# Operands of a Winograd-style product: one by one for all tokens, on VectorE, with four units started ahead

## The chip, the cores and the metric

The kernel runs on one core of a Trainium2 chip. The metric is the device time of one execution in microseconds (us). The time before is 3162.38 us, the median of three runs.

The core's engines each work an instruction queue of their own in order: TensorE (PE in the rows; its weight loads are PEld), VectorE (DVE), ScalarE (ACT), GpSimd (POOL) and SyncE (SP), which here only issues DMAs. They wait for one another by semaphores.

## The reference

One transformer-like block of two different attentions, then a second block of two layers, over 1024 tokens of 1024 features, all in fp32. The change concerns the second block only, at the place where the mixer of a layer ends and its MLP begins:

```python
def sq_relu_mlp(h, w1, w2):
    return jnp.square(jax.nn.relu(h @ w1)) @ w2

for layer in range(DEPTH_2):                     # 2 layers
    if layer < N_A_LAYERS:
        mix = s5_mixer(h, ...)                   # ends in (val * sigmoid(gate)) @ w_out
    else:
        mix = mla_mixer(h, ...)                  # ends in o @ w_o
    h = layer_norm(DN_ALPHA * h + mix, ln_mix_g[layer], ln_mix_b[layer])
    h = layer_norm(DN_ALPHA * h + sq_relu_mlp(h, w_ff1[layer], w_ff2[layer]), ln_ffn_g[layer], ln_ffn_b[layer])
```

`w1` is 1024 x 4096 and `w2` is 4096 x 1024.

## The kernel before

**Precision.** Every fp32 matrix is used as two parts: a high part, rounded to the format that PE multiplies (fp32r), and the rest. `split` (L155 to L159) makes them: L157 copies the high part on ACT, L159 subtracts it from the source on an engine that the caller chooses (GpSimd if it names none). A product then takes three matmuls: high by high, high by low, low by high.

**`lin_ln`** (L1186) is the last projection of a layer's mixer. It goes over eight token tiles of 128 tokens, in two column halves `ch`. With the second half a tile's row is complete: it is added to the residual (L1215), normalized (`ln`, L1143 to L1154, the last step on DVE is L1154), written to memory (L1221) and transposed (`to_T4`: L1176 on PE, L1177 on ACT) into the pages `B[K, hf, pr]`: `K` is the feature half, `hf` the token half (tiles 0 to 3 or 4 to 7), `pr` one of two pairs of tiles in it. So for each `pr` there are four pages of 128 x 1024, called b11, b12 (K 0, the two token halves), b21, b22 (K 1).

**Seven products in place of eight.** The first MLP matmul is a 2 x 2 block product done with seven block products (Winograd's form of Strassen's method). The moving operands are sums of the blocks: X1 = b11, X2 = b21, X3 = b22, X5 = t1 = b12 - b11, X6 = t2 = b22 - t1, X7 = b22 - b12, X4 = b21 - t2. Each X[p] is kept for 512 tokens as a high and a low part in two pages of 256 features each (`split_T`), so each X takes, for each `pr`, two splits of 128 x 512 elements. X1 and X2 are split as soon as a pair of tiles of the first token half is done. The others are made after the last tile, in a loop over `pr` (L1236 to L1251): differences L1239, L1240 and L1244 on DVE and L1242 on GpSimd; the splits of X6, X5 and X4 on DVE, those of X1, X2, X7 and X3 on GpSimd.

**`ff1_unit`** (L1260) is a generator for one pair of feature tiles, 16 of which (*units*) make the first MLP matmul of a layer. A unit loads two weight pages of 512 KB: `r0` (L1293), whose split gives the weights of products 1 and 2, and `r1` (L1272), from which with `r0` the sums of `sums()` are made (L1273 to L1276 on DVE, their splits on ACT and GpSimd) for the other five. A product is 12 matmuls of 512 columns (`product`, L1257). Products 1 and 2 need X1 and X2 alone. The order of a unit's products is 1, 2, 6, 7, 5, 4, 3; L1304, L1308, L1317, L1323, L1327, L1332 and L1340 read their results from PSUM.

**Order.** Units 0 and 1 are started early inside `lin_ln`, at tiles 4 and 6, and do products 1 and 2 before the last operands are there (`early`); they use PSUM banks 4 and 5 for them. From unit 2 on, `ff1` (L1346) always starts the next unit's loads and sums while a unit is worked on. The code gives the engines' order only in part: Tile's scheduler may put an instruction ahead of others whose data come later. Pages come from a common list of free ones; a page that is given back is taken again by whoever asks next, who then waits for its last reader.

## Time and profile before

| | us |
|---|---|
| median of three runs | 3162.38 (3157.11 to 3164.09) |
| the profiled execution's own time | 3152.57 |
| its span | 3150.8 |
| PE busy | 3002.2 (95%) |
| DVE busy | 1705.4 (54%) |
| ACT busy | 1106.6 (35%) |
| POOL busy | 1464.0 (46%) |

The mean granted TensorE clock of the profiled execution is 0.98 of full speed. The change's two places in time are the transitions from `lin_ln` to `ff1`, at 1304 to 1350 us in layer 0 and at 2452 to 2498 us in layer 1. In the rows, a releaser behind `<-` names the instruction whose end let the waiting one start, and a group x24 counts 24 instructions that follow each other without another between them.

### The profile page before, as it was taken

To read this page: it belongs to the slowest core of one execution; us is meant where nothing else is said; L and a number is where in the kernel's file an instruction comes from. 1 tells how busy PE (TensorE), PEld (TensorE's weight loads), DVE (VectorE), ACT (ScalarE), POOL (GpSimd) and SP (SyncE) were. 2 spreads that over 40 slices of the span, in tenths; PEclk is the share of its full clock that TensorE was granted. 3 is DMA by queue.
4 is the path that set the end of the run, shared out by engine and by line. 5 is a ranking of instruction groups with operands and counts; after the bars stand their busy time and mean duration, and the time that the engine had idled before them with its cause. 6 is when DMAs were issued, how large, how long until landed. Compare 5 with 4: busy or idle time off the path is not lost.

```text
span 3150.8 us, 38281 instructions
## 1 busy us (share of the span) xinstructions
PE 3002.2 (95%) x14764; PEld 2473.2 (78%) x14764; DVE 1705.4 (54%) x2466; ACT 1106.6 (35%) x1723; POOL 1464.0 (46%) x871
## 2 busy tenths in 40 slices
PE   8999889999998899799999999999999799999998
PEld 6777667777777788678888888879998588888887
DVE  7555547755289301854444464765554854444446
ACT  4332247765223211332232221346562332232110
POOL 5455537644523232654455443513354654464442
PEclk9999999999999999899999999999999899999999
DMA  4353462476544122223363231111132133362211
GB/s 169 134 173 110 131 202 81 131 211 215 192 143 133 41 67 94 79 95 111 114 227 120 98 107 61 69 45 45 44 114 96 68 113 107 110 243 102 104 71 74
DMA packets 165014, 365.75 MB, mean 116 GB/s; under 512 B 21568, under 2 KB 70976, under 8 KB 164832
## 3 DMA queue, kind: packets, MB, share of 16 engines
q1 hardware_dynamic: 164688, 363.18, 34.0%
q8 instruction: 116, 1.90, 0.2%
q14 instruction: 66, 0.54, 0.1%
q10 hardware_dynamic: 144, 0.13, 0.0%
HBM read 248.70 MB, written 106.17 MB: 113 GB/s over the span
## 4 chain that ended last, share of the span: by engine, by line
PE 77%; DVE 12%; DMA 4%; POOL 2%; issue 2%; ACT 2%; SPq 1%; DVEq 0%; POOLq 0%; ACTq 0%
PE ps L172 56%; PE ps L1257 17%; DMA dr<-p 2%; POOL p L159 1%; DVE p L159 1%; DVE p L1032 1%; PE ps L1625 1%; DVE p L1045 1%; DMA p<-in_w_ff 1%; PE ps L668 1%; DVE p L498 1%; DVE p L1154 1%; PE ps L521 1%; POOL rsd L180 1%; ACT p L500 1%
## 5 line engine op out<-in xcount | busy, mean ns | idle before, releaser
L172 PE MATMUL ps<-p,p 128*128 128x512 f32 (+6 forms) x10520 | 2237.3, 373 | 63.1 <-POOL p L159 11.7
L172 PEld LDWEIGHTS ps<-p,p 128*128 128x128 f32 (+2 forms) x10520 | 1790.1, 185 | 438.4 <-issue 50.7
L159 POOL TENSOR_TENSOR p<-p,p 128x1024 fp32r<-128x1024 f32 (+2 forms) x436 | 982.3, 2274 | 955.3 <-ACT p L157 673.9
L157 ACT ACTIVATE p<-p 128x1024 fp32r<-128x1024 f32 (+2 forms) x462 | 423.9, 939 | 957.6 <-DMA p<-in_w_ff 452.9
L1257 PE MATMUL ps<-p,p 128*128 128x512 f32 x2688 | 622.1, 393 | 32.5 <-ACT p L157 31.6
L1257 PEld LDWEIGHTS ps<-p,p 128*128 128x128 f32 x2688 | 506.5, 189 | 146.6 <-ACT p L157 36.3
L1402 DVE SCALAR_TENSOR_TENSOR p<-ps,p 128x1024 f32<-128x1024 f32 x247 | 301.3, 1223 | 335.4 <-PE ps L172 335.4
L180 POOL TENSOR_TENSOR rsd<-rst,nhalf 128x1 f32<-128x1 f32 (+1 forms) x64 | 103.3, 1615 | 200.3 <-DVE rst L178 200.2
L1290 DVE SCALAR_TENSOR_TENSOR p<-p 128x512 f32<-128x512 f32 x96 | 96.9, 1010 | 2.5
L498 DVE CUSTOM_DVE_ANT_0 p<-ps,bw 128x1024 f32<-128x1024 f32 x64 | 77.3, 1220 | 30.6 <-PE ps L172 21.6
L1124 DVE SCALAR_TENSOR_TENSOR p<-p,ps 128x1024 f32<-128x1024 f32 x8 | 9.8, 1221 | 142.1 <-ACT p L1123 142.1
L500 ACT ACTIVATE p<-p,m 128x1024 f32<-128x1024 f32 x64 | 73.4, 1148 | 31.1 <-DVE m L498 19.5
L1619 POOL TENSOR_SCALAR p<-p,rz 128x256 f32<-128x256 f32 (+6 forms) x64 | 49.0, 766 | 65.3 <-DVE rz L1618 63.8
L1340 DVE TENSOR_TENSOR p<-p,ps 128x512 f32<-128x512 f32 x32 | 22.0, 688 | 104.5 <-PE ps L1257 104.4
L513 POOL TENSOR_TENSOR p<-p,p 128x1024 f32<-128x1024 f32 x32 | 76.9, 2407 | 2.0
L512 POOL TENSOR_SCALAR p<-p,c 128x1024 f32<-128x1024 f32 x32 | 37.2, 1163 | 84.8 <-DMA dr<-p 43.5
L1308 DVE TENSOR_TENSOR p<-p,ps 128x512 f32<-128x512 f32 x32 | 22.0, 686 | 97.2 <-PE ps L1257 97.0
L665 POOL TENSOR_SCALAR p<-p,rz 128x384 f32<-128x384 f32 x64 | 38.4, 604 | 68.8 <-DVE rz L664 54.2
L1629 DVE TENSOR_TENSOR p<-ps,p 128x512 fp32r<-128x512 f32 (+3 forms) x96 | 50.8, 553 | 32.5 <-ACT p L1628 31.8
L1614 POOL CAST p<-zeros 128x128 fp32r<-128x128 f32 x64 | 18.4, 298 | 105.4 <-PE ps L172 71.1
L159 DVE TENSOR_TENSOR p<-ps,p 128x1024 fp32r<-128x1024 f32 (+1 forms) x42 | 42.1, 1020 | 36.8 <-ACT p L157 34.0
L1177 ACT ACTIVATE p<-ps 128x512 f32<-128x512 f32 x32 | 17.8, 595 | 123.6 <-PE ps L1176 123.5
(255 smaller groups left out, 2420.2 us busy)
## 6 DMA issues: line engine op xcount, KB each, us to landing
p<-dr SPq DMA_DIRECT2D x174, 512.0 KB
dr<-p SPq DMA_DIRECT2D x158, 512.0 KB
p<-in_w_ff SPq DMA_DIRECT2D x128, 512.0 KB
bw<-in_rpbw SPq DMA_DIRECT2D x16, 768.0 KB
dr<-p SPq DMA_DIRECT2D x80, 128.0 KB
p<-p SPq DMA_DIRECT2D x64, 128.0 KB
p<-dr SPq DMA_DIRECT2D x32, 256.0 KB
p<-in_w_glu SPq DMA_DIRECT2D x16, 512.0 KB
```

The lines of the kernel that those rows point to most:

```text
L157: nc.scalar.activation(hi, src, AF.Copy, scale=scale)
L159: (eng or nc.gpsimd).tensor_tensor(lo, src, hi.bitcast(F32), SUB)
L172: self.nc.tensor.matmul(out, l, r, start=start, stop=stop)
L180: nc.gpsimd.tensor_tensor(dst, t, self.nhalf[:, :n], ALU.pow)
L498: V.tensor_tensor_reduce(out=s.t, in0=ps, in1=bw[:, 896 - 128 * t:1920 - 128 * t], scale=-1.0, scalar=3e38, op0=ADD, op1=ALU.min, accum_ou ...
L500: A.activation(s.t, s.t, AF.Exp, bias=m[:, c:c + 1], scale=-1.0, accum_out=z[:, c:c + 1])
L513: G.tensor_tensor(p[0].t, p[0].t, p[1].t, ADD)
L1257: self.nc.tensor.matmul(ps, w[a][:, kt, :], x[b][kt // 2].t[:, kt % 2, :], start=start and kt == 0 and (a, b) == (0, 0), stop=kt == 3 and ...
L1290: V.scalar_tensor_tensor(h, h, 0.0, h, ALU.max, MUL)
L1402: V.scalar_tensor_tensor(z[t].t, ps, IALPHA, z[t].t, MUL, ADD)
L1619: G.tensor_scalar(s.t[:, :n], s.t[:, :n], rz, 1.0, MUL, MUL)
L1629: V.tensor_tensor(atl[kq][:, :nb, qi * 128:(qi + 1) * 128], tv, oh.bitcast(F32), SUB)
```

## The change

The blocks b11 to b22 become lists over `pr`. A helper `op` makes one operand for both `pr` at once, first the two differences, then the four splits, in the order X6, X7, X5, X4, X3; t1 is made in place in b11. Everything that GpSimd did for the operands (X1, X2, X7 and X3's splits and the difference of X7) is done on DVE. Units 2 and 3 become early too: with units 0 and 1 they do products 1 and 2 inside `lin_ln`, in PSUM banks 4, 5, 0 and 1. The low part of units 2 and 3's first weights is made on DVE; an early unit gives `r0` back after its split and loads it a second time before `sums()`. In `ff1` units 1 to 3 make their sums when their turn comes, and the next unit's loads are started ahead from unit 4 on.

```diff
--- before.py
+++ after.py
@@ -1201,7 +1201,7 @@
         units = deque()
         for ch in range(2):
             ws = ws if ch == 0 else nat(1)
-            self.psum(**(dict(g1=[0, 1], tr=[2, 3], P=[4, 5], Q=[6, 7]) if ch else dict(g1=range(8))))
+            self.psum(**(dict(g1=[0, 1], tr=[2, 3], P=[4, 5, 0, 1], Q=[6, 7]) if ch else dict(g1=range(8))))
             for t in range(8):
                 ps = self.bank("g1")
                 hf, sl = t // 4, slice(t % 4 * 128, (t % 4 + 1) * 128)
@@ -1227,27 +1227,46 @@
                     self.fr(z[t])
                     if hf == 0 and t % 2:
                         for K in range(2):
-                            self.split_T(B[K, 0, pr].t, X, 1 + K, pr, G)
+                            self.split_T(B[K, 0, pr].t, X, 1 + K, pr, V)
                     if t in (4, 6):
                         units.append(self.ff1_unit(j, t // 2 - 2, X, True))
                         next(units[-1])
             self.fr(*(p for w in ws for p in w.pg))
         self.fr(*gb)
-        for pr in range(2):
-            b11, b12, b21, b22 = (B[K, hf, pr] for K in range(2) for hf in range(2))
-            t1, t2 = self.pg((128, 4, 256)), self.pg((128, 4, 256))
-            V.tensor_tensor(t1.t, b12.t, b11.t, SUB)
-            V.tensor_tensor(t2.t, b22.t, t1.t, SUB)
-            self.split_T(t2.t, X, 6, pr, V)
-            G.tensor_tensor(b12.t, b22.t, b12.t, SUB)
-            self.split_T(b12.t, X, 7, pr, G)
-            V.tensor_tensor(b21.t, b21.t, t2.t, SUB)
-            self.split_T(t1.t, X, 5, pr, V)
-            self.split_T(b21.t, X, 4, pr, V)
-            self.split_T(b22.t, X, 3, pr, G)
-            self.fr(b11, b12, b21, b22, t1, t2)
-            next(units[pr])
-            next(units[pr])
+        b11, b12, b21, b22 = ([B[K, hf, pr] for pr in range(2)] for K in range(2) for hf in range(2))
+        t2 = [self.pg((128, 4, 256)) for _ in range(2)]
+
+        def op(p, o, x, y):
+
+            for pr in range(2):
+                if y is not None:
+                    V.tensor_tensor(o[pr].t, x[pr].t, y[pr].t, SUB)
+            for pr in range(2):
+                if p:
+                    self.split_T(o[pr].t, X, p, pr, V)
+
+        def first(k):
+
+            for _ in range(2):
+                next(units[k])
+
+        op(0, b11, b12, b11)
+        op(6, t2, b22, b11)
+        first(0)
+        first(1)
+        op(7, b12, b22, b12)
+        self.fr(*b12)
+        for k in (2, 3):
+            units.append(self.ff1_unit(j, k, X, True))
+            next(units[k])
+            first(k)
+        next(units[0])
+        op(5, b11, None, None)
+        self.fr(*b11)
+        op(4, b21, b21, t2)
+        self.fr(*b21, *t2)
+        op(3, b22, None, None)
+        self.fr(*b22)
         return X, units
 
     def product(self, ps, w, x, start):
@@ -1292,7 +1311,9 @@
         r0 = self.pg()
         nc.sync.dma_start(r0.t, self.i["w_ff1"][layer, 2 * i])
         w0 = [self.pg(dt=F32R) for _ in range(2)]
-        self.split(r0.t, w0[0].t, w0[1].t)
+        self.split(r0.t, w0[0].t, w0[1].t, eng=V if early and i > 1 else None)
+        if early:
+            self.fr(r0)
         yield
         if not early:
             w23, w14, w4 = sums()
@@ -1310,6 +1331,8 @@
         self.fr(*w0)
         yield
         if early:
+            r0 = self.pg()
+            nc.sync.dma_start(r0.t, self.i["w_ff1"][layer, 2 * i])
             w23, w14, w4 = sums()
             yield
         self.product(P, [kv(w.t[:, lo]) for w in w23], X[6], False)
@@ -1345,13 +1368,13 @@
 
     def ff1(self, X, units, layer):
 
-        self.psb.update({"P": cycle([0, 1, 4, 5]), "R": cycle([2, 3])})
+        self.psb["R"] = cycle([2, 3])
         prev = None
         for i in range(16):
             u = units.popleft()
-            for _ in range(1 if i < 2 else 2):
+            for _ in range((0, 1, 1, 1)[i] if i < 4 else 2):
                 next(u)
-            nxt = self.ff1_unit(layer, i + 1, X, False, i == 14) if 0 < i < 15 else None
+            nxt = self.ff1_unit(layer, i + 1, X, False, i == 14) if 2 < i < 15 else None
             if nxt:
                 units.append(nxt)
                 next(nxt)
```

The new code has the operands' differences in line 1243, the product's matmuls in 1276, the first load of `r0` in 1312 and the second in 1335, `r1` in 1291, the weight sums in 1292 to 1295.

PE, layer 0, around the transposes (L1176) of the last token tile, whose normalized row is `p_888`. Before, unit 1's products (weights `p_925`, `p_926`) end there and unit 0's product 6 (operand `p_929`, `p_931`, weights `p_958`) comes next:

```order
L1257 MATMUL ps<-p_912_8999,p_926_9244 128x512
L1257 MATMUL ps<-p_912_8999,p_925_9243 128x512
L1257 MATMUL ps<-p_914_9001,p_925_9243 128x512
L1257 MATMUL ps<-p_912_8999,p_926_9244 128x512
L1176 MATMUL ps<-ident,p_888_8660 128x128 x8
L1257 MATMUL ps<-p_929_9294,p_958_9427 128x512
L1257 MATMUL ps<-p_931_9296,p_958_9427 128x512
L1257 MATMUL ps<-p_937_9312,p_960_9431 128x512
L1257 MATMUL ps<-p_939_9314,p_960_9431 128x512
L1257 MATMUL ps<-p_929_9294,p_959_9428 128x512
```

And now, where `p_940` and `p_941` are unit 2's weights, `p_944` and `p_945` unit 3's, and `p_907` to `p_914` hold X1 and X2, `p_956` X5:

```order
L1276 MATMUL ps<-p_912_8999,p_941_9381 128x512
L1276 MATMUL ps<-p_912_8999,p_940_9380 128x512
L1276 MATMUL ps<-p_914_9001,p_940_9380 128x512
L1276 MATMUL ps<-p_912_8999,p_941_9381 128x512
L1176 MATMUL ps<-ident,p_888_8660 128x128 x8
L1276 MATMUL ps<-p_907_8990,p_944_9414 128x512
L1276 MATMUL ps<-p_909_8992,p_944_9414 128x512
L1276 MATMUL ps<-p_911_8998,p_944_9414 128x512
L1276 MATMUL ps<-p_913_9000,p_944_9414 128x512
L1276 MATMUL ps<-p_956_9467,p_953_9460 128x512
```

The transposes now stand behind unit 2's products 1 and 2, and unit 3's come after them, ahead of everything that needs the other operands.

DVE, layer 0, the end of the row of operands before: `p_943` and `p_944` are X4's low parts, `p_931` and `p_932` X6's, L1273 to L1276 unit 0's weight sums:

```order
L159 TENSOR_TENSOR p_940_9315<-p_950_9364,p_938_9313 128x2x256
L1244 TENSOR_TENSOR p_916_9045<-p_916_9045,p_951_9365 128x1024
L1274 TENSOR_TENSOR p_956_9420<-p_957_9421,p_919_9147 128x512
L159 TENSOR_TENSOR p_931_9296<-p_951_9365,p_929_9294 128x2x256
L159 TENSOR_TENSOR p_932_9297<-p_951_9365,p_930_9295 128x2x256
L1276 TENSOR_TENSOR p_957_9421<-p_919_9147,p_956_9420 128x512
L159 TENSOR_TENSOR p_943_9322<-p_916_9045,p_941_9320 128x2x256
L159 TENSOR_TENSOR p_944_9323<-p_916_9045,p_942_9321 128x2x256
```

And now, with X4's low parts in `p_962` and `p_963`, X3's in `p_966` and `p_967`:

```order
L159 TENSOR_TENSOR p_966_9495<-p_918_9141,p_964_9493 128x2x256
L159 TENSOR_TENSOR p_966_9495<-p_923_9235,p_964_9493 128x2x256
L159 TENSOR_TENSOR p_967_9496<-p_918_9141,p_965_9494 128x2x256
L159 TENSOR_TENSOR p_967_9496<-p_923_9235,p_965_9494 128x2x256
L159 TENSOR_TENSOR p_963_9484<-p_916_9045,p_961_9482 128x2x256
L1293 TENSOR_TENSOR p_973_9565<-p_974_9566,p_971_9562 128x512
L1309 SCALAR_TENSOR_TENSOR p_946_9418<-p_946_9418 128x512
L159 TENSOR_TENSOR p_962_9483<-p_906_8941,p_960_9481 128x2x256
L159 TENSOR_TENSOR p_962_9483<-p_916_9045,p_960_9481 128x2x256
```

X3's four splits came from POOL and stand ahead of X4's last three.

POOL, layer 0, the same stretch before (`p_917`, `p_922`: X7; `p_945` to `p_948`: X3; L180: the root of the normalization):

```order
L159 TENSOR_TENSOR p_947_9330<-p_918_9141,p_945_9328 128x2x256
L1242 TENSOR_TENSOR p_917_9135<-p_918_9141,p_917_9135 128x1024
L159 TENSOR_TENSOR p_948_9331<-p_918_9141,p_946_9329 128x2x256
L159 TENSOR_TENSOR p_936_9306<-p_917_9135,p_934_9304 128x2x256
L159 TENSOR_TENSOR p_935_9305<-p_917_9135,p_933_9303 128x2x256
L180 TENSOR_TENSOR rsd_8930<-rst_8928,nhalf 128x1
L159 TENSOR_TENSOR p_962_9435<-p_955_9419,p_962_9435 128x512
L1242 TENSOR_TENSOR p_922_9229<-p_923_9235,p_922_9229 128x1024
L159 TENSOR_TENSOR p_947_9330<-p_923_9235,p_945_9328 128x2x256
L159 TENSOR_TENSOR p_948_9331<-p_923_9235,p_946_9329 128x2x256
L159 TENSOR_TENSOR p_935_9305<-p_922_9229,p_933_9303 128x2x256
L159 TENSOR_TENSOR p_936_9306<-p_922_9229,p_934_9304 128x2x256
```

And now, with only weights left (`p_952` to `p_955` unit 0's sums, `p_976` to `p_979` unit 1's):

```order
L159 TENSOR_TENSOR p_921_9150<-p_919_9147,p_920_9149 128x1024
L180 TENSOR_TENSOR rsd_8930<-rst_8928,nhalf 128x1 x4
L159 TENSOR_TENSOR p_952_9457<-p_949_9449,p_951_9456 128x1024
L180 TENSOR_TENSOR rsd_8930<-rst_8928,nhalf 128x1
L159 TENSOR_TENSOR p_955_9464<-p_948_9448,p_955_9464 128x512
L159 TENSOR_TENSOR p_954_9461<-p_950_9450,p_953_9460 128x1024
L159 TENSOR_TENSOR p_979_9580<-p_972_9564,p_979_9580 128x512
L159 TENSOR_TENSOR p_976_9573<-p_973_9565,p_975_9572 128x1024
L159 TENSOR_TENSOR p_978_9577<-p_974_9566,p_977_9576 128x1024
```

The operands' splits and differences are gone from POOL's row, and the weight splits of unit 0 and unit 1 follow each other.

## Rows read from the trace of the kernel before

**Rows 1.** Windows: stretch, length, busy us (count) per engine, PEclk, DMA share, GB/s.

```profile
1304.00:1350.00 46.00, 23.41 (x91) 17.52 (x89) 44.96 (x37) 17.80 (x31) 29.30 (x17) 0.70 0.16 58
1350.00:1360.00 10.00, 9.78 (x42) 7.54 (x43) 1.63 (x2) 3.44 (x5) 7.06 (x3) 1.00 0.16 52
```

**Rows 2.** PE's timeline, layer 0: start, us, operation [idle before <-releaser].

```profile
1302.20 2.09 PE L172 MATMUL ps<-p,p 128*128 128x512 f32 x8
...
1306.92 1.04 PE L1176 MATMUL ps<-ident,p 128*128 128x128 f32 x8
1307.71 8.52 PE L1257 MATMUL ps<-p,p 128*128 128x512 f32 x36
1323.40 1.94 PE L1176 MATMUL ps<-ident,p 128*128 128x128 f32 x8 [7.16 <-DVE p L1154]
1339.99 9.30 PE L1257 MATMUL ps<-p,p 128*128 128x512 f32 x24 [14.65 <-ACT p L157]
1349.92 0.73 PE L1257 MATMUL ps<-p,p 128*128 128x512 f32 x2 [0.63 <-ACT p L157]
```

**Rows 3.** The chain that ended last: start, us, link; layer 0's transition.

```profile
1277.76 4.89 DMA dr<-p
...
1350.87 273.61 PE ps L1257 x1198
```

**Rows 4.** PE's timeline, layer 1, the same three waits.

```profile
2471.88 1.94 PE L1176 MATMUL ps<-ident,p 128*128 128x128 f32 x8 [7.32 <-DVE p L1154]
2488.43 8.56 PE L1257 MATMUL ps<-p,p 128*128 128x512 f32 x24 [14.60 <-ACT p L157]
2498.31 0.72 PE L1257 MATMUL ps<-p,p 128*128 128x512 f32 x2 [1.32 <-ACT p L157]
```

**Rows 5.** Groups on DVE, 1304 to 1350: busy us, mean ns | idle before.

```profile
L159 DVE TENSOR_TENSOR p<-p,p 128x512 fp32r<-128x512 f32 x12 | 16.4, 1393 | 0.1
...
L1240 DVE TENSOR_TENSOR p<-p,p 128x1024 f32<-128x1024 f32 x2 | 6.8, 3422 | 0.1
...
L1273 DVE TENSOR_TENSOR p<-p 128x512 f32<-128x512 f32 x2 | 3.5, 1756 | 0.0
...
L1244 DVE TENSOR_TENSOR p<-p,p 128x1024 f32<-128x1024 f32 x2 | 3.5, 1746 | 0.0
...
L1239 DVE TENSOR_TENSOR p<-p,p 128x1024 f32<-128x1024 f32 x2 | 2.4, 1216 | 0.0
...
L1274 DVE TENSOR_TENSOR p<-p,p 128x512 f32<-128x512 f32 x2 | 1.4, 678 | 0.0
```

**Rows 6.** Groups on POOL and ACT, 1304 to 1350.

```profile
L159 POOL TENSOR_TENSOR p<-p,p 128x512 fp32r<-128x512 f32 x10 | 17.3, 1745 | 1.6 <-ACT p L157 1.6
...
L159 POOL TENSOR_TENSOR p<-p,p 128x1024 fp32r<-128x1024 f32 x3 | 7.7, 2569 | 6.3 <-ACT p L157 6.3
...
L1242 POOL TENSOR_TENSOR p<-p,p 128x1024 f32<-128x1024 f32 x2 | 5.2, 2624 | 7.5 <-ACT p L157 5.2 <-DVE p L1239 2.3
...
L157 ACT ACTIVATE p<-p 128x1024 fp32r<-128x1024 f32 x4 | 4.1, 1050 | 7.3 <-DVE p L1274 7.0 <-DVE p L1276 0.3
```

**Rows 7.** DVE's timeline, two places.

```profile
1304.11 2.31 DVE L1154 SCALAR_TENSOR_TENSOR p<-p,rsd,p 128x1024 f32<-128x1024 f32 x1 [0.44 <-POOL rsd L180]
...
1338.33 1.28 DVE L159 TENSOR_TENSOR p<-p,p 128x512 fp32r<-128x512 f32 x2
```

**Rows 8.** SyncE's queue: the issue of one weight load.

```profile
1336.75 0.33 SPq L1272 DMA_DIRECT2D p<-in_w_ff  x1
```

**Rows 9.** POOL's timeline, three places.

```profile
1307.63 2.41 POOL L1242 TENSOR_TENSOR p<-p,p 128x1024 f32<-128x1024 f32 x1 [2.30 <-DVE p L1239]
...
1320.25 1.26 POOL L159 TENSOR_TENSOR p<-p,p 128x512 fp32r<-128x512 f32 x1
...
1349.94 7.12 POOL L159 TENSOR_TENSOR p<-p,p 128x1024 fp32r<-128x1024 f32 x3 [2.98 <-ACT p L157]
```

**Rows 10.** Windows: a stretch elsewhere, columns as in group 1.

```profile
1003.00:1013.00 10.00, 5.98 (x53) 4.49 (x50) 9.89 (x11) 3.48 (x7) 5.35 (x4) 0.96 0.18 54
```

## The prediction

> **What bounds the kernel now.** I read the chain of waits first. From 1350.87 us on it is one stretch of 273.61 us of block products, 1198 matmuls without another engine between them [rows 3]: once `ff1` is under way the matrix engine (PE) alone sets the pace, and nothing of this change can help there. Then the busy time by windows: in the 46 us before that, PE works 23.41 us, VectorE (DVE) 44.96, GpSimd (POOL) 29.30, and the granted clock is 0.70 [rows 1]. So the transition from `lin_ln` to `ff1` is bound by DVE, and PE waits. PE's timeline says for what [rows 2]: 7.16 us before the last token tile's transposes (releaser L1154 on DVE, the tile's normalization), 14.65 us before the first X6 product (its weights' or operand's split, L157 on ACT, which itself follows the differences), then 0.63. That is 22.4 us of idle PE. After it 24 matmuls take 9.30 us, where 36 took 8.52 us before, 0.2367 each: 24 × 0.2367 = 5.68, so the fallen clock costs 3.6 us more. Loss of this transition: 26.0 us. The second layer repeats it [rows 4]: 7.32 + 14.60 + 1.32 = 23.2 idle, 8.56 − 5.68 = 2.9 for the clock, 26.1 in all. Both together, 52.1 us of 3152.57, are all that the change can reach; it touches nothing else.
>
> **The change, part by part.** (a) **PE gets work for the wait.** Units 2 and 3 do products 1 and 2 there too: 48 more matmuls of the 0.2367 kind, 11.4 us, moved forward from `ff1`, not added. In the new order there stand, from unit 0's first product to the first use of X4, 134 matmuls (96 of the four units' first two products, 12 each on X5, X6, X7, two of unit 1's X6) and three groups of transposes (0.79 us each, 1307.71 − 1306.92 [rows 2]). The stretch begins at 1303.5: the end of L172's last piece, 1302.20 + 2.09 = 1304.3, less one transpose group, which now stands further back. 134 × 0.2367 = 31.7, and 2.4 of transposes: PE at full clock wants X4 at 1337.6.
>
> (b) **DVE gets the work that POOL had.** Of each transition 16 splits of 512 elements (X1, X2, X7, X3) and two differences of 1024 go from POOL to DVE. Clean prices on DVE: 0.60 per 512 (two in 1.28 where the last shows 0.68 [rows 7]) and 1.22 per 1024 (L1239's mean, 1.216 [rows 5]); 16 × 0.60 + 2 × 1.22 = 12.0 us. X1's and X2's eight, 4.8 us of it, fall before the stretch, while PE still has the projection's matmuls: I take nothing for them (4.8 is their upper bound). The rest I count with the queue. DVE works its queue in order: from the normalization of tile 6, which starts at 1304.11 [rows 7] and takes 1.2, to the last split of X4 there now stand 51 instructions: 12 of 1024 (eight differences, two normalization steps, two weight splits) × 1.22 = 14.6; 37 of 512 (20 splits of operands, the rest weight sums, evictions, squares) × 0.60 = 22.2; two small ones 0.4. That ends at 1342.5 if nothing disturbs it.
>
> (c) **What POOL still does to DVE.** Something does disturb it now: L1240, a difference like L1239, takes 3.422 us on average against 1.216, and the 12 splits of L159 take 1.393 against 0.678 for L1274 of the same size [rows 5]. L159, L1240, L1273 and L1244 take 16.4 + 6.8 + 3.5 + 3.5 = 30.2 us, and by the clean 0.678 and 1.216 they should take 14 × 0.678 + 4 × 1.216 = 14.4: 15.8 us are lost while POOL runs 15 tensor instructions that read the same memory, ten, three and two [rows 6], 1.05 us lost per POOL instruction. In the trace DVE seems to stand still while POOL's instruction runs. (The Trainium skill, "SBUF — State Buffer", section "Who interferes with whom", states it as an exclusive lock on a shared port pair, for a DVE instruction with two SBUF inputs against a GpSimd one that reads SBUF; rows 5 agree with it.) In the new order four POOL splits are left in the stretch, two of 1024 and two of 512. Undisturbed such ones take about 2.41 (L1242, the same size) and 1.26 us [rows 9]. If each holds DVE for its whole length: 2 × 2.41 + 2 × 1.26 = 7.3; at the rate of now, 4 × 1.05 = 4.2. I take 7.3, since DVE has no gap in this stretch that could take one up. X4 is ready at 1349.8.
>
> (d) **The gap.** 1349.8 − 1337.6 = 12.2 us of idle PE (9.1 with 4.2). It will not lie before X4 alone: X5, X6 and X7 come some 10 to 16 DVE instructions before it, so PE waits before X5 first. The clock then costs between 0 and the 3.6 of now; PE's pauses are shorter, and I take 1.5. New loss 13.7, gain 26.0 − 13.7 = 12.3 per transition.
>
> (e) **Waits that this absorbs.** Tile 7's transposes now stand behind three units' products: 72 × 0.2367 + 1.6 after 1303.5 is 1322; L1154 of tile 7 ends on DVE near 1324.5 (some 15 us of queue and half of the POOL time after 1305.3), so PE waits some 2.5 us there, in place of 7.16, and since it is early for X5 in any case this adds nothing. Unit 3's weights are split into a page that tile 7's row write gives back: 1324.5 + 4.89 for such a write [rows 3] + 1.05 on ACT [rows 6] is 1330.4; 62 matmuls follow to X4, 14.7 us: 1345.1, before 1349.8, at nothing. If the write took 5 us longer it would begin to cost. On the queue of SyncE four more weight loads of 512 KB per layer are issued (the page of each early unit's first weights is given back and read again before its sums); the stretch uses 0.16 of the DMA engines [rows 1], so I put them at nothing, and what they cost if they are late is rival C.
>
> **Rivals.** **E, the clock.** If PE's pauses leave it at the lower of its two levels (1.2 of 2.4 GHz) for 20 of the 31.7 us, PE reaches X4 at 1357.6, after DVE: loss 20, gain 6 per transition, 3150. For it: 0.70 in the stretch now. Against: in a stretch elsewhere with PE 5.98 us of 10 busy the granted clock was 0.96 [rows 10]. **B, DVE is full already.** DVE is 44.96 of 46 us busy [rows 1] and is given more. If it loses as much to POOL as now (15.8 in place of 7.3), X4 comes at 1358.3, the gap is 20.7, with the clock's 3.6 the loss 24.3, gain 1.7 per transition, 3159: no change that can be told. Against it: POOL has four instructions there where it has 15. (The Trainium skill, "Perfetto Trace Analysis", section "Optimizing Scalar/DVE Operations", would rather have it the other way: move work off a saturated DVE to ScalarE or GpSimd; by that rule the time would be B's 3159. The same section adds that GpSimd and DVE share a read port, so that such a move may not help, which is what rows 5 show.) **C, slower: the weights of units 1 to 3 come late.** Their sums are no longer prepared a unit ahead. From the issue of such a load to the end of its last split takes 1336.75 [rows 8] to 1349.94 + 7.12 = 1357.06 [rows 9], 20.3 us; PE has 60 matmuls, 14.2 us, per unit to cover it in `ff1`. If none of it is prefetched, 6.1 us are late in each of three units, 18.3: loss 32.0, 6.0 slower per transition, 3174. It decides from 12.3 / 3 = 4.1 us per unit on. Against it: in the order unit 1's loads stand before X4, and in the 10 us after 1350 DVE has only 1.63 us of work [rows 1], so the chain can run ahead. That the change does not do what it says is no rival: the order shows the 96 matmuls in place.
>
> **How the numbers follow.** 2 × 12.3 = 24.6; the profiled execution is 9.8 us under the median of 3162.38, and the gain is the same for both: 3162.4 − 24.6 = 3137.8, 3138 (profiled, 3128). Chances: forecast 0.63; better still (locks 4.2, clock 0, X1 and X2 free: loss 9.1, gain 16.9 each, 3128.6) 0.07; E 0.11; B 0.10; C 0.09. Faster by over 0.2% (6.3 us, about what a measurement of this kernel can tell from no change) are the first three: 0.81; same 0.10; slower 0.09. The range reaches from the better case, with a microsecond and a half for the sum's own roughness, past E: 3127 to 3155, leaving out B and C.
>
> **What would show it.** In the new profile, from 1303 on: PE with three or four groups of block products before tile 7's transposes, and an idle time of 2 to 3 us there; then 10 to 12 us of idle before the products of X5 to X4, released by splits, not by a DMA; DVE without gap from 1304 to about 1350, and its L159 of 512 at a mean near 0.8 us, not 1.39; POOL with four splits in that stretch. B shows as a mean still near 1.4 us; E as a clock below 0.7 with PE busy throughout; C as idle PE after 1350, inside `ff1`, released by splits or loads of units 1 to 3. If the idle time is neither before X5 to X4 nor there, the sum is wrong in its basis.

## The result

| | us | against the kernel before |
|---|---|---|
| forecast | 3138.0 (3127 to 3155) | 24.6 less |
| first comparison, median of 4 runs | 3125.78 (3122.45 to 3131.40) | ratio 0.989, 95% interval 0.9872 to 0.9909; 35.8 less than 3161.61 |
| `again`, 5 runs | 3129.51 | 0.9903 (0.9887 to 0.9919), 30.1 less than 3159.58 |
| `again_2`, 4 runs | 3129.68 | 0.9911 (0.9896 to 0.9927), 27.8 less than 3157.48 |

The changed kernel is faster, by about 1%. The forecast had the sign and most of the mechanism, but too little of the gain: the first median lies 1.2 us below its range. The two later ones lie inside it, and they too show more gain than forecast. Why 24.6 was too small, and why the three comparisons differ, is taken up below.

PE's timeline of the changed kernel, layer 0 (start, us, operation, [idle before and what ended it]; L1276 are the block products, L1176 the transposes):

```profile
1305.59 0.40 PE L1276 MATMUL ps<-p,p 128*128 128x512 f32 x1
1305.83 1.03 PE L1176 MATMUL ps<-ident,p 128*128 128x128 f32 x8
1306.62 4.84 PE L1276 MATMUL ps<-p,p 128*128 128x512 f32 x20
1311.30 1.03 PE L1176 MATMUL ps<-ident,p 128*128 128x128 f32 x8
1312.09 6.90 PE L1276 MATMUL ps<-p,p 128*128 128x512 f32 x29
1319.40 2.59 PE L1276 MATMUL ps<-p,p 128*128 128x512 f32 x10 [0.42 <-DVE p L159]
1322.23 3.02 PE L1276 MATMUL ps<-p,p 128*128 128x512 f32 x12 [0.24 <-DVE p L1329]
1325.09 1.04 PE L1176 MATMUL ps<-ident,p 128*128 128x128 f32 x8
1328.44 1.49 PE L1276 MATMUL ps<-p,p 128*128 128x512 f32 x4 [2.31 <-ACT p L157]
1334.00 0.80 PE L1276 MATMUL ps<-p,p 128*128 128x512 f32 x1 [4.07 <-ACT p L157]
1335.68 12.25 PE L1276 MATMUL ps<-p,p 128*128 128x512 f32 x43 [0.88 <-DVE p L159]
1348.61 3.48 PE L1276 MATMUL ps<-p,p 128*128 128x512 f32 x14 [0.69 <-ACT p L1340]
1352.37 270.60 PE L1276 MATMUL ps<-p,p 128*128 128x512 f32 x1186 [0.28 <-ACT p L1346]
```

Where PE stood idle for 22.4 us in three long pieces [rows 2], it now idles 8.89 us in seven short ones (0.42, 0.24, 2.31, 4.07, 0.88, 0.69, 0.28). The transposes of the last tile, which waited 7.16 us for L1154, come at 1325.09 without a wait: 72 products stand before them. The largest wait is 4.07 us, for a split on ACT (L157); the single matmul behind it is the first on X5, whose second pair's split comes last. From 1352.37 on PE works 270.60 us without a wait, as it did from 1350.87 [rows 3].

By windows of 46 us over both transitions (columns as in [rows 1]):

```profile
1306.00:1352.00 46.00, 37.38 (x157) 28.56 (x155) 43.59 (x53) 23.30 (x39) 11.97 (x7) 0.89 0.22 77
2440.00:2486.00 46.00, 37.44 (x158) 28.34 (x156) 43.57 (x53) 23.57 (x40) 12.21 (x7) 0.89 0.21 76
```

PE does 37.38 us of work in the stretch where it did 23.41, POOL 11.97 in place of 29.30, and DVE is as full as before, 43.59 (44.96 [rows 1]). The mean granted clock is 0.89, not 0.70.

The groups on DVE that answer to [rows 5], layer 0, 1306 to 1352 (L1243 are the differences; L159 the low parts; us busy, mean ns):

```profile
L159 DVE TENSOR_TENSOR p<-p,p 128x512 fp32r<-128x512 f32 x20 | 14.9, 787 | 0.0
L1243 DVE TENSOR_TENSOR p<-p,p 128x1024 f32<-128x1024 f32 x8 | 12.9, 1629 | 0.0
```

DVE's 512-element splits take 787 ns on average where they took 1393, and there are 20 in place of 12. L1243 still has a mean of 1629 ns against the clean 1216. DVE's timeline has three places where it loses time (1312.38, 1319.27 and 1324.51), and, at its end, the last split of X4; the other lines are used further down. POOL's timeline of the same stretch follows it:

```profile
1306.24 1.28 DVE L1154 SCALAR_TENSOR_TENSOR p<-p,rsd,p 128x1024 f32<-128x1024 f32 x1 [0.44 <-POOL rsd L180]
...
1312.38 4.58 DVE L1243 TENSOR_TENSOR p<-p,p 128x1024 f32<-128x1024 f32 x2
...
1319.27 2.31 DVE L1243 TENSOR_TENSOR p<-p,p 128x1024 f32<-128x1024 f32 x1
...
1324.51 3.44 DVE L159 TENSOR_TENSOR p<-p,p 128x512 fp32r<-128x512 f32 x2
...
1332.07 1.21 DVE L1243 TENSOR_TENSOR p<-p,p 128x1024 f32<-128x1024 f32 x1
...
1334.41 1.21 DVE L159 TENSOR_TENSOR p<-p,p 128x1024 fp32r<-128x1024 f32 x1
...
1347.98 1.28 DVE L159 TENSOR_TENSOR p<-p,p 128x512 fp32r<-128x512 f32 x2
```

```profile
1311.83 2.91 POOL L159 TENSOR_TENSOR p<-p,p 128x1024 fp32r<-128x1024 f32 x1 [5.62 <-ACT p L157]
...
1318.59 1.91 POOL L159 TENSOR_TENSOR p<-p,p 128x512 fp32r<-128x512 f32 x1
1324.73 2.67 POOL L159 TENSOR_TENSOR p<-p,p 128x1024 fp32r<-128x1024 f32 x1 [4.22 <-DVE p L1154]
1349.16 7.03 POOL L159 TENSOR_TENSOR p<-p,p 128x512 fp32r<-128x512 f32 x3 [21.76 <-ACT p L157]
```

Each of the three places has a POOL split of weights beside it: 4.58 us for two differences that take 2.35 alone (1335.55, further down the same timeline, shows two in 2.35), 2.31 for one that takes 1.21, 3.44 for two splits that take 1.28. Together 5.5 us are lost beside 7.5 us of POOL work.

### The profile page after: what moved, and what is told of

The parts are those of the page before. It is cut to its first block, busy times and chain, and to the rows that moved or that the text cites. A ratio compares the mean times of both kernels' runs of the same rounds, so it can differ in the third digit from the quotient of the medians.

```text
span 3123.3 us, 38309 instructions
## 1 busy us (share of the span) xinstructions
PE 3002.7 (96%) x14764; PEld 2471.2 (79%) x14764; DVE 1688.7 (54%) x2506; ACT 1106.9 (35%) x1723; POOL 1388.0 (44%) x831
## 4 chain that ended last, share of the span: by engine, by line
PE 77%; DVE 11%; DMA 4%; issue 2%; POOL 2%; ACT 2%; SPq 0%; DVEq 0%; POOLq 0%; ACTq 0%
PE ps L172 56%; PE ps L1276 18%; DMA dr<-p 2%; POOL p L159 1%; PE ps L1648 1%; DMA p<-dr 1%; DVE p L1032 1%; DMA p<-in_w_ff 1%; DVE p L159 1%; DVE p L1045 1%; PE ps L668 1%; DVE p L498 1%; POOL rsd L180 1%; PE ps L521 1%; ACT p L500 1%
## 5 line engine op out<-in xcount | busy, mean ns | idle before, releaser
L172 PE MATMUL ps<-p,p 128*128 128x512 f32 (+6 forms) x10520 | 2238.1, 373 | 64.4 <-POOL p L159 12.1
L172 PEld LDWEIGHTS ps<-p,p 128*128 128x128 f32 (+2 forms) x10520 | 1790.5, 186 | 440.2 <-issue 50.1
L159 POOL TENSOR_TENSOR p<-p,p 128x1024 fp32r<-128x1024 f32 (+2 forms) x400 | 917.8, 2314 | 997.7 <-ACT p L157 687.9
L157 ACT ACTIVATE p<-p 128x1024 fp32r<-128x1024 f32 (+2 forms) x462 | 423.8, 939 | 935.8 <-DMA p<-in_w_ff 442.9
L1276 PE MATMUL ps<-p,p 128*128 128x512 f32 x2688 | 624.9, 393 | 17.6 <-ACT p L157 12.6
L1276 PEld LDWEIGHTS ps<-p,p 128*128 128x128 f32 x2688 | 506.4, 189 | 133.4 <-ACT p L157 14.1
L180 POOL TENSOR_TENSOR rsd<-rst,nhalf 128x1 f32<-128x1 f32 (+1 forms) x64 | 102.9, 1610 | 219.7 <-DVE rst L178 219.6
L498 DVE CUSTOM_DVE_ANT_0 p<-ps,bw 128x1024 f32<-128x1024 f32 x64 | 77.4, 1220 | 30.6 <-PE ps L172 21.9
L1309 DVE SCALAR_TENSOR_TENSOR p<-p 128x512 f32<-128x512 f32 x96 | 90.3, 940 | 2.4
L500 ACT ACTIVATE p<-p,m 128x1024 f32<-128x1024 f32 x64 | 73.4, 1148 | 30.6 <-DVE m L498 19.4
L159 DVE TENSOR_TENSOR p<-ps,p 128x1024 fp32r<-128x1024 f32 (+1 forms) x42 | 42.3, 1017 | 38.6 <-ACT p L157 35.7
```

The source lines that it names most:

```text
L157: nc.scalar.activation(hi, src, AF.Copy, scale=scale)
L159: (eng or nc.gpsimd).tensor_tensor(lo, src, hi.bitcast(F32), SUB)
L172: self.nc.tensor.matmul(out, l, r, start=start, stop=stop)
L180: nc.gpsimd.tensor_tensor(dst, t, self.nhalf[:, :n], ALU.pow)
L498: V.tensor_tensor_reduce(out=s.t, in0=ps, in1=bw[:, 896 - 128 * t:1920 - 128 * t], scale=-1.0, scalar=3e38, op0=ADD, op1=ALU.min, accum_ou ...
L500: A.activation(s.t, s.t, AF.Exp, bias=m[:, c:c + 1], scale=-1.0, accum_out=z[:, c:c + 1])
```

## The experiments

All of them undo or do one part; what each one is stands below, under its expectation. To compare them by place and not by the whole time, I take from each profile the **loss of a transition**: from the start of the matmul of L172 that lies 150 before `lin_ln`'s last one to the start of the 300th block product, less the work in between at steady prices (150 matmuls of L172 at 0.2294 us, 64 transposes at 0.0987, 300 block products at the mean of the 400th to the 1200th of the same layer, 0.227 to 0.229). It counts idle time and slow clock together.

| kernel | ratio to before (95%) | us less (medians) | loss in layer 0, layer 1 |
|---|---|---|---|
| before | 1 | | 28.8, 28.6 |
| order_only | 0.9990 (0.9979 to 1.0002) | 5.1 | 29.6, 28.9 |
| sums_only | 0.9981 (0.9972 to 0.9989) | 4.3 | 26.6, 26.4 |
| engine_only | 0.9974 (0.9962 to 0.9985) | 6.6 | 25.4, 26.8 |
| early_only | 0.9968 (0.9956 to 0.9980) | 9.0 | 24.0, 23.9 |
| two_units | 0.9967 (0.9955 to 0.9980) | 9.8 | 21.1, 26.1 |
| pool_again | 0.9958 (0.9945 to 0.9972) | 14.6 | 23.6, 23.7 |
| late_sums | 0.9954 (0.9940 to 0.9967) | 14.5 | 21.6, 21.7 |
| engine_sums | 0.9933 (0.9920 to 0.9947) | 23.4 | 19.6, 19.6 |
| pair_loop | 0.9929 (0.9917 to 0.9942) | 21.7 | 19.0, 19.1 |
| changed (again) | 0.9903 (0.9887 to 0.9919) | 30.1 | 13.3, 13.5 |
| five_first | 0.9879 (0.9865 to 0.9892) | 37.1 | 12.0, 12.4 |

**The changed kernel again.**

> The changed kernel once more, on another chip beside the kernel before. Theory 1 (the mechanism is as forecast, 12.4 us per transition, and the rest of the 35.8 us between the first medians is the state in which the runs of before happened to be): 25 to 30 us less than before. Theory 2 (the change gives something more that one profiled execution of before does not show): 34 to 38 us less again.

30.1 us less. The interval of the ratio overlaps with that of the first comparison. By transitions, the first profile of the changed kernel loses 14.2 and 13.8 us, this one 13.3 and 13.5, against 28.8 and 28.6: 29.4 and 30.6 us less in all. Theory 1 it is, at its upper end; its 12.4 us per transition were too little, since I had read them off the absolute times of two profiles, in which the changed kernel enters the transition 2.4 us later (first transposes at 1272.49 and 1270.14).

**One part alone.** First the engine: the operands' work on DVE, in the old loop.

```diff
-                            self.split_T(B[K, 0, pr].t, X, 1 + K, pr, G)
+                            self.split_T(B[K, 0, pr].t, X, 1 + K, pr, V)
-            G.tensor_tensor(b12.t, b22.t, b12.t, SUB)
-            self.split_T(b12.t, X, 7, pr, G)
+            V.tensor_tensor(b12.t, b22.t, b12.t, SUB)
+            self.split_T(b12.t, X, 7, pr, V)
-            self.split_T(b22.t, X, 3, pr, G)
+            self.split_T(b22.t, X, 3, pr, V)
```

> The kernel before, with the splits of X1, X2, X7, X3 and the difference of X7 on DVE; order and early units as before. Locks theory (DVE stands still while POOL reads the same memory, 15.8 us per transition): 12 us of work come to DVE, 7.2 of them in the stretch, and 11 us of standing still go, so 3 to 5 us less per transition, 6 to 10 us in all. Rival (DVE is simply full, the slow instructions are slow for another reason): 7 us more per transition, 14 us slower.

6.6 us less; 3.4 and 1.8 us per transition. More work on DVE made the kernel faster: the rival by which DVE is simply full falls. But the profile shows something that was not expected. DVE, ACT and PE at the end of the wait in engine_only (lines as before the change: L1274 is a weight sum, L1240 and L1244 differences of operands, L159 a split):

```profile
1331.04 2.50 DVE L159 TENSOR_TENSOR p<-p,p 128x512 fp32r<-128x512 f32 x4
1333.44 0.69 DVE L1274 TENSOR_TENSOR p<-p,p 128x512 f32<-128x512 f32 x1
```

```profile
1334.17 1.06 ACT L157 ACTIVATE p<-p 128x1024 fp32r<-128x1024 f32 x1 [1.86 <-DVE p L1274]
```

```profile
1335.28 1.22 PE L1257 MATMUL ps<-p,p 128*128 128x512 f32 x2 [14.86 <-ACT p L157]
```

The operands X6 are split by then (X6 and X5 of the second pair at 1331.04), and PE still waits 14.86 us, as long as before. What it waits for is the copy on ACT of a weight sum, L1274, which DVE made at 1333.44: unit 0's sums stand behind the operands in DVE's queue, and product 6 needs both. This is theory S of the next runs.

Then the four early units alone:

```diff
+        for k in (2, 3):
+            units.append(self.ff1_unit(j, k, X, True))
+            next(units[k])
+            first(k)
+        next(units[0])
```

(behind the old loop, with the changes to `ff1_unit`, `ff1` and the banks that belong to it.)

> The kernel before, with four early units only; the operands are made in the loop over the pairs and partly on POOL as before. If the work moved forward for PE is what pays: 11.4 us of matmuls less the about 5 us that DVE does more (two weight splits, four evictions and squares), so 5 to 8 us less per transition, 10 to 16 in all. If the gain is DVE's alone: no change or some us slower.

9.0 us less, 4.8 per transition: a little under the expected 5 to 8. And the order alone, in the place of the old loop (with `op` as in the change, but the engine as its last argument):

```diff
+        op(0, b11, b12, b11)
+        op(6, t2, b22, b11)
+        first(0)
+        first(1)
+        op(7, b12, b22, b12, G)
+        op(5, b11, None, None)
+        op(4, b21, b21, t2)
+        op(3, b22, None, None, G)
```

> The kernel before, with the operands made one by one for all tokens, engines and early units as before. X6 is complete some 5 us earlier, but X4 no earlier: PE waits later instead. Expected within 5 us of before by either theory; a gain of 10 us or more would make the order the cause.

No difference that can be told (the interval holds 1), and no gain in the transitions.

**Sums of what is alone do not make the whole.** engine_only, early_only and order_only take 3.4 + 4.8 − 0.8 = 7.4 us off layer 0's loss; the change takes some 15. (By the medians the three add up to 20.7 of 30.1 us, but each median's difference is uncertain by some 4 us.) The rest had to be in what the parts do together. The next four runs test theory S.

```diff
         for k in (2, 3):
             units.append(self.ff1_unit(j, k, X, True))
             next(units[k])
             first(k)
-        next(units[0])
         op(5, b11, None, None)
...
-            for _ in range((0, 1, 1, 1)[i] if i < 4 else 2):
+            for _ in range(1 if i < 4 else 2):
```

> The changed kernel, with unit 0's weight sums called at unit 0's turn in ff1, as before the change, and no longer ahead of the operands X5, X4 and X3. Theory S (product 6 waits for two things made one after the other on DVE, the operand X6 and unit 0's weight sums; whichever is moved alone leaves the other): less than half of the gain is left, 10 to 15 us less than before in all. Theory F (the sum of the forecast, in which the sums' place is no term: matmuls moved forward and DVE freed of the waits on POOL): 25 to 30 us less, as the changed kernel.

14.5 us less, half of the gain is gone. PE's wait, what ACT and DVE did at its end, and SyncE's issue of unit 0's second weight page:

```profile
1354.87 1.22 PE L1275 MATMUL ps<-p,p 128*128 128x512 f32 x2 [12.61 <-ACT p L157]
```

```profile
1353.76 1.06 ACT L157 ACTIVATE p<-p 128x1024 fp32r<-128x1024 f32 x1 [2.37 <-DVE p L1292]
```

```profile
1350.76 0.69 DVE L1291 TENSOR_TENSOR p<-p 128x512 f32<-128x512 f32 x1 [1.55 <-DMA p<-in_w_ff]
```

```profile
1347.43 1.53 SPq L1290 DMA_DIRECT2D p<-in_w_ff  x2
```

One wait of 12.61 us is back, ended by the copy of a sum (L157 at 1353.76, itself released by L1292, a sum in this kernel's lines); the load of the weights (`in_w_ff`) lands only at 1350.76. Theory F falls: the place of one line, `next(units[0])`, carries 7.9 us of loss per transition (21.6 to 13.7, the mean of the changed kernel's traces). But the way is not quite that of theory S. Here the sums do not stand behind operands in DVE's queue: DVE had been idle for 1.55 us before the first of them (L1291), and waited for the load, which SyncE issued only at 1347.43, after waiting 13.1 us for a split on DVE, presumably for a page that this split gave back. A late call thus makes the sums late in two ways, through DVE's queue (engine_only) and through the pages.

Now the other way round, the kernel before with the sums' place alone, and the same with the engine too:

```diff
+        for k in (0, 0, 1, 1, 0):
+            next(units[k])
         for pr in range(2):
...
-            next(units[pr])
-            next(units[pr])
```

> The kernel before, with unit 0's weight sums called ahead of the loop over the pairs and nothing else changed (operands partly on POOL, two early units). Theory S: product 6 then waits for the operand alone, which the locks make late: 2 to 3 us less per transition at most, 3 to 6 us in all. If the late sums alone were the cause of the wait: 14 or more.

4.3 us less, 2.2 per transition. What product 6 waits for is now an operand: in this kernel L159 on DVE makes operands alone.

```profile
1337.69 8.25 PE L1257 MATMUL ps<-p,p 128*128 128x512 f32 x25 [6.04 <-DVE p L159]
```

> The kernel before, with the operands' work on DVE as in engine_only, and unit 0's weight sums called ahead of the loop over the pairs; two early units, loop over pairs as before. Theory S: 7 to 8 us less per transition, 14 to 17 in all, where engine_only gave 7. Theory F: 6 to 8 in all, as engine_only.

23.4 us less by the medians, 21 by the ratio, 9.1 per transition in the traces, more than theory S expected: with the engine and the sums' place together three fifths of the gain in the traces are there, without units 2 and 3 and without the new order. Each of the two alone gives 2 to 3 us, both together 9: product 6 needs the later of two things, and whoever moves one of them leaves the other.

The changed kernel with the four calls of the operands that were POOL's on POOL again:

```diff
-        op(7, b12, b22, b12)
+        op(7, b12, b22, b12, G)
-        op(3, b22, None, None)
+        op(3, b22, None, None, G)
```

(and `G` for X1 and X2's splits.)

> The changed kernel, with X1, X2, X7 and X3's splits and the difference of X7 back on POOL. Theory S with the locks (DVE stands still while POOL reads): more than half of the gain goes, 11 to 15 us less than before. If the engine were no matter: 29. If POOL's help were worth more than its locks: above 30.

14.6 us less. The same groups in its stretch read, below that of PE's products:

```profile
L1276 PE MATMUL ps<-p,p 128*128 128x512 f32 x127 | 37.4, 453 | 14.1 <-DVE p L159 8.2 <-ACT p L157 5.9
...
L159 DVE TENSOR_TENSOR p<-p,p 128x512 fp32r<-128x512 f32 x12 | 13.9, 1194 | 0.0
...
L1243 DVE TENSOR_TENSOR p<-p,p 128x1024 f32<-128x1024 f32 x6 | 10.6, 1762 | 0.0
```

DVE has eight splits and two differences less to do there, and what is left takes longer: its 512-element splits have a mean of 1194 ns where the changed kernel has 787. PE's waits there end on DVE and on ACT, none on POOL. The loss is 23.6 in place of 14. The Trainium skill ("Perfetto Trace Analysis", section "Optimizing Scalar/DVE Operations") says that offloading some work from a saturated DVE to ScalarE or even GpSimd may make sense, and that between GpSimd and DVE it might not help, since the two share an SBUF read port. Here the run agrees with the second of these: with this work on GpSimd the kernel takes 15 us more. The port itself is in no trace.

The changed kernel with the old loop over the pairs:

```diff
-        op(0, b11, b12, b11)
...
-        op(3, b22, None, None)
+        for pr in range(2):
...
+            self.split_T(b22.t, X, 3, pr, V)
```

> The changed kernel, with the operands made in the loop over the pairs as before, on DVE; four early units, unit 0's sums behind that loop in the code. Both theories: X5, X7 of the second pair come later, 9 to 10 us less per transition, 18 to 20 in all. If the order were the main cause, no more than 10 in all.

21.7 us less, the loss is 19.0 where the changed kernel has 13.7. So the new order, with the place behind X7 that it gives to unit 0's sums (here they stand behind the whole loop), is worth 5 us per transition when the rest is there; the order alone is worth nothing.

And with units 2 and 3 left where they were before:

```diff
-        for k in (2, 3):
-            units.append(self.ff1_unit(j, k, X, True))
-            next(units[k])
-            first(k)
         next(units[0])
```

(and `ff1_unit`, `ff1` and the PSUM banks as before the change.)

> The changed kernel with two early units in place of four (operands one by one on DVE, unit 0's sums ahead of X5, X4 and X3; the loads and sums of later units as before the change). Theory S: the operands and sums come as early as in the changed kernel, but PE has 48 matmuls less to fill the wait, 11 us; some of the wait goes with DVE's smaller load: 13 to 18 us less than before in all. If units 2 and 3 were no matter: 29.

9.8 us less, short of what was expected. Layer 0 loses 21.1 us, 7.3 more than the changed kernel, where 11 were expected for the 48 matmuls. Layer 1 loses 26.1. There DVE stood still 5.44 us before a weight sum whose load was late:

```profile
2481.59 2.48 DVE L159 TENSOR_TENSOR p<-p,p 128x512 fp32r<-128x512 f32 x4
2489.51 0.69 DVE L1288 TENSOR_TENSOR p<-p 128x512 f32<-128x512 f32 x1 [5.44 <-DMA p<-in_w_ff]
```

SyncE issued this load at 2486.31, after waiting 13.0 us for a split on POOL, and that split was a long one:

```profile
2477.83 8.45 POOL L159 TENSOR_TENSOR p<-p,p 128x1024 fp32r<-128x1024 f32 x1 [8.71 <-ACT p L157]
```

In layer 0 the split in this place took 2.79 us (1335.95), and the load went out at 1338.77. The long one ended at 2486.28, 2.2 us after DVE's run of splits (2481.59 + 2.48 = 2484.07). So the 9.8 us mix two things, and layer 0's 7.3 is the cleaner measure of what units 2 and 3 are worth.

**A faster one.** Since the longest wait left was for X5 of the second pair, and X5 needs one difference only, it was made before X6, behind the products and sums that need no operand:

```diff
-        op(0, b11, b12, b11)
-        op(6, t2, b22, b11)
         first(0)
         first(1)
+        next(units[0])
+        op(0, b11, b12, b11)
+        op(5, b11, None, None)
+        self.fr(*b11)
+        op(6, t2, b22, b11)
         op(7, b12, b22, b12)
```

(with `next(units[0])` and `op(5, ...)` taken out further down.)

> A try at a faster one: the changed kernel, with units 0 and 1's products and unit 0's sums called ahead of all operands, and X5 made ahead of X6 (it needs one difference only), since in the trace of the changed kernel PE's longest wait, 4.07 us, is for an X5 split of the second pair. Theory S: the split comes some 4 us sooner: 3 us less per transition than the changed kernel, 5 to 7 us less in all. If X4's end sets the time: no change against it.

37.1 us less than before. PE's timeline from the wait for X5 on:

```profile
1334.81 0.50 PE L1276 MATMUL ps<-p,p 128*128 128x512 f32 x1 [2.62 <-ACT p L157]
1337.13 7.91 PE L1276 MATMUL ps<-p,p 128*128 128x512 f32 x23 [1.81 <-ACT p L157]
...
1349.42 15.93 PE L1276 MATMUL ps<-p,p 128*128 128x512 f32 x68 [0.69 <-ACT p L1346]
```

The wait for X5 has gone from 4.07 to 2.62 us. From its first product PE is at X4 after 44.1 us (1349.42 − 1305.31) and 132 products, where the changed kernel took 46.8 us for 134; the two products are worth 0.46 us, so 2.2 us are gained there. The loss is 12.0 and 12.4 us, some 1.8 us less per transition than in the changed kernel's traces, where 3 were expected. What is left stands on ACT, which waited 6.99 us for POOL ahead of the copies for X5 and X6 in its queue:

```profile
1333.12 0.63 ACT L157 ACTIVATE p<-p 128x512 fp32r<-128x512 f32 x1 [6.99 <-POOL p L159]
```

POOL's split was itself held up. It took 10.47 us, where those of its size in the changed kernel's stretch took 2.67 and 2.91, and ended at 1333.09, 2.24 us after DVE, busy until then, had run out of work at 1330.85 (1328.50 + 2.35):

```profile
1322.63 10.47 POOL L159 TENSOR_TENSOR p<-p,p 128x1024 fp32r<-128x1024 f32 x1 [8.39 <-ACT p L157]
```

```profile
1328.50 2.35 DVE L1243 TENSOR_TENSOR p<-p,p 128x1024 f32<-128x1024 f32 x2
1333.79 2.17 DVE L159 TENSOR_TENSOR p<-p,p 128x512 fp32r<-128x512 f32 x1 [2.93 <-ACT p L157]
```

A second try starts one of the loads earlier as well:

```diff
-                    if t in (4, 6):
+                    if t in (4, 6, 7):
```

(with unit 2 taken out of the later loop.)

> As five_first, and unit 2's first weights loaded and split at the last token tile, not after the operands: 0 to 1 us per transition less than five_first.

34.6 us less (0.9887, 0.9871 to 0.9902), losses 11.5 and 11.4: not to be told from five_first by the time, half a microsecond to a whole one better in the traces.

> The changed kernel a third time, beside the kernel before and five_first on one chip. The two comparisons so far gave 35.8 (four runs each) and 30.1 us less than before. By the transitions of the traces, 14.7 us each, it is 29 to 31 again; if the first comparison was the true one, 34 to 38.

> five_first beside the changed kernel on one chip: by the transitions of its trace 3 to 4 us less each, 6 to 8 us less than again_2 in all. If its first result was the chip's: within 2 us of again_2.

27.8 us less for the changed kernel, a little under the 29 to 31 expected, and 34.1 for five_first (0.9892, 0.9875 to 0.9909) on the same chip: 6.3 us between the two medians, as expected, though their intervals overlap. The traces show less: a mean loss of 13.8 us in six transitions of the changed kernel (14.2, 13.8, 13.3, 13.5, 13.6, 14.3), 12.0 in four of five_first (12.0, 12.4, 11.1, 12.5), so 3.6 us in all. That five_first is the faster one is likely, by how much is open.

## Why the forecast came out as it did

**What bounds the kernel: the reading was right, its sum was too small.** This is the step that failed: the loss of a transition, 26.0 and 26.1 us in the forecast, is 28.1 and 28.0. The forecast's 26.0 us adds three idle times and one slow group. The same rows give more when one takes elapsed time less work: from 1304.3 to 1350.87 [rows 2, 3] are 46.6 us; the work in it is 74 products at the steady 273.61 / 1198 = 0.2284, 16.9 us, and two groups of transposes at 0.79, 1.6 us. The rest is 28.1. What the list left out: the transposes at 1323.40 took 1.94 us at the low clock in place of 0.79; the last two products 0.73 in place of 0.46; 0.22 idle at 1350.87 (in the timeline, not among the rows); and it priced the 24 slow matmuls, and took the 36 before them, at 0.2367, a mean with start-up in it, not at the 0.2284 that PE holds afterwards. For layer 1, the rows of before that frame the stretch, and those of the changed kernel:

```profile
2450.70 2.07 PE L172 MATMUL ps<-p,p 128*128 128x512 f32 x8
...
2499.26 11.07 PE L1257 MATMUL ps<-p,p 128*128 128x512 f32 x47 [0.23 <-ACT p L157]
```

```profile
2439.65 0.39 PE L1276 MATMUL ps<-p,p 128*128 128x512 f32 x1
...
2486.03 24.16 PE L1276 MATMUL ps<-p,p 128*128 128x512 f32 x104 [0.29 <-ACT p L1346]
```

From 2452.8 to 2499.26 are 46.5 us, less the same 18.5 of work 28.0, where the forecast had 26.1. These 2.1 and 1.9 us are nearly the whole of what the forecast lacked against the traces: 24.6 forecast, 28.9 by these sums (14.3 and 14.6 with the next paragraph), 29.4 and 30.6 by the losses that the traces gave above. The rest of what the first comparison shows beyond the forecast stands in no transition, and is taken up at the end of this section.

**The loss that remains came out as forecast, but made of other parts.** By the same sum the changed kernel loses, from its first product at 1305.59 to 1352.37, 46.8 less 134 × 0.2284 + 3 × 0.79 = 33.0: 13.8 us; in layer 1, 46.4 − 33.0 = 13.4. The forecast had 13.7. Of these, 8.9 are idle time, where 12.2 was forecast, and 4.9 are slow clock and start-ups, where 1.5 was: that the total agrees is luck, since two errors of over 3 us cancel. Both errors are of one step, (d): PE was to wait for X4's last split, and it did not. That split ended at 1349.26 (1347.98 + 1.28), 43.0 us after L1154 of tile 6 began, where the forecast had 45.7: three POOL splits fell into the stretch, not four, and cost 5.5 us, not 7.3, and the 1024-element instructions follow at 1.14, not 1.22. PE got to X4 at 1352.37, after it, at a mean pitch of 0.285 for 43 matmuls (12.25 us), of which those before 1340.5 ran at the lower clock (0.50 granted).

**(e), the cover for unit 3's weights, was gone.** The forecast set them at nothing, since they would be there by 1330.4 with 62 matmuls to go. Their high part was there at 1328.39 (1327.33 + 1.06), two us sooner than that, but PE was ready for it sooner still and waited 2.31 us; it was held up as said, by tile 7's row write:

```profile
1327.33 1.06 ACT L157 ACTIVATE p<-p 128x1024 fp32r<-128x1024 f32 x1 [0.52 <-DMA dr<-p]
```

Their low part is one of DVE's two weight splits and stood in its queue until 1334.41 (+ 1.21); PE waited 0.88 for it at 1335.68, behind the 4.07 for X5, whose difference DVE began at 1332.07. From there 57 matmuls were left to X4. So the time was set at 1335.68, by rows in the middle of DVE's queue, and not by the end of it; five_first moves X5's rows forward, and some 1.8 us per transition follow. The forecast did say that PE would wait before X5 first, but did not price it.

**(c), the waits on POOL, were right in kind and a third too large.** POOL's three splits cost DVE 5.5 us in 7.5 of their own time; the forecast took four and the whole of their time, 7.3. engine_only and pool_again show the same from both sides: given more work DVE makes PE wait less, given less it is slower at what is left and PE waits more. That DVE can hold up POOL in turn (10.47 and 8.45 us for a split, above) the forecast did not have; in the changed kernel's stretch it does not show.

**What the forecast did not see is that it needed the sums' new place.** It wrote of the 14.65 us that it was for the first X6 product's "weights' or operand's split", and left open which. It was both at nearly the same time, in the kernel before:

```profile
1337.73 0.68 DVE L1274 TENSOR_TENSOR p<-p,p 128x512 f32<-128x512 f32 x1
```

```profile
1337.84 2.10 ACT L157 ACTIVATE p<-p 128x512 fp32r<-128x512 f32 x3 [5.03 <-DVE p L1244]
```

X6's last low part was done at 1339.61 (1338.33 + 1.28 [rows 7]), and the third of these copies, that of the weight sum which L1274 completes, at 1339.94; PE began at 1339.99. The change moves both. Because the order of the changed kernel was counted row by row, the sums were in the count in the right place, and the result did not suffer; but the reasons given, matmuls moved forward and DVE freed from POOL, would have been a wrong forecast for late_sums, which has both and gains 14.5 us.

**What was to be seen.** DVE without a gap to 1350 (it is, to 1349.8) and its 512-element splits near 0.8 us (787 ns) came as written; POOL has three splits in the stretch, not four; the idle time of 2 to 3 us lies behind tile 7's transposes, not before them; before the products of X5 to X4 PE idles 5.9 us (4.07 + 0.88 + 0.69 + 0.28), not 10 to 12.

**The rivals.** E: the clock was low for some 10 of 46 us (0.89 of full on the mean, with levels of 1 and 0.5), not for 20. B: DVE's 512-element splits have a mean of 787 ns; it would have needed 1.4 us. C: no wait of PE after 1352.37, though DVE waited 2.65 us for a weight load there once, at 1356.59, which PE did not notice.

**The first comparison's 35.8 us** hold 5 to 8 us that no place in the two transitions shows, and that two further comparisons do not repeat. What they are is not settled. Chance is enough for them: the 95% interval of that comparison reaches from 40.5 down to 28.8 us less, and that this kernel's executions vary by as much elsewhere is shown below. With the 29.4 us of the transitions the first median would have been 3132.2, inside the range; that it fell outside is in part luck.

## What to carry to other kernels

Price a wait by elapsed time less work at the pace that the engine holds afterwards, not by adding up the idle times that a view lists: slow groups, start-ups and clock fall through such a list. When a wait ends with two inputs that come at nearly the same time, name both and what each waits for, since moving one gives little and both together a multiple (2 to 3 us and 9 here). And a helper engine that reads the same memory can cost the main one as much time as it saves, or be held up by it: work taken from POOL and given to a full DVE made it finish sooner.

## What the runs showed of the hardware

**DVE and POOL hold each other up.** In the changed kernel 7.5 us of POOL splits cost DVE 5.5 us, and POOL's 1024-element splits took 2.67 and 2.91 us. In five_first and in layer 1 of two_units it was POOL that stood: such splits took 10.47 and 8.45 us, and both ended some 2.2 us after DVE's run of work had stopped. What decides which of the two goes first no run here separates.

**The clock outside the change.** The first matmul group after a wait of some 8 us in the first block, which no version here touches, in the kernel before and in order_only:

```profile
328.29 14.70 PE L172 MATMUL ps<-p,p 128*128 128x512 f32 x53 [8.32 <-POOL p L159]
```

```profile
330.85 18.04 PE L172 MATMUL ps<-p,p 128*128 128x512 f32 x53 [8.41 <-POOL p L159]
```

The same 53 matmuls take 14.70 us in the one execution and 18.04 in the other; the mean granted clock over them is 0.84 and 0.66, a mix of the two levels 1 and 0.5 (2.4 and 1.2 GHz). From the first matmul of L172 to the 3001st, all in unchanged code, the traces of these kernels take between 771.4 us (sums_only) and 784.7 (late_sums), 775.3 in the kernel before. Executions of the kernel before on one chip lie between 3153.17 and 3167.29 us. So a difference of 10 us between two single executions needs no cause in the change, and a profile's whole span tells less than its transitions do.
